# Turning attention weights and rows with VectorE and transfers in place of TensorE transposes

## The chip, the cores and the metric

The kernel runs on one core of a Trainium2 chip. A core has a matrix engine (TensorE, PE in the profile), a vector engine (VectorE, DVE), a scalar engine (ScalarE, ACT), a general engine (GpSimd, POOL) and a synchronisation engine (SyncE, SP). Each works through its own list of instructions in order; semaphores make one wait for another. SP issues the transfers of the weights; POOL issues those of intermediate data. The metric is the device time of one execution in microseconds.

## The reference

One decoder layer on 256 tokens of 2048 channels, in float32: a half-step gated feed-forward network (FFN), a token mixer of two attention branches, a second FFN, each followed by a layer norm.

```python
h = _layer_norm(ALPHA * x + 0.5 * _swiglu(x, ...), ...)
# mixer, with c_q, c_kv, k_r, dq, dk, dv, gate_mla, gate_diff = columns of h @ w_in
q = _rms_norm(c_q) @ w_uq              # 8 heads of 128, and 64 more that are rotated
k_nope, v = _rms_norm(c_kv) @ w_uk, _rms_norm(c_kv) @ w_uv
o_mla = softmax(q k^T * scale, causal) @ v                                   # 8 heads
o_diff = (softmax(s1) - lam * softmax(s2)) @ dv                              # 4 heads, 256 wide
o_diff = _rms_norm(o_diff, subln_g) * (1 - lambda_init)
y = sigmoid(gate_mla) * (o_mla @ w_br_mla) + sigmoid(gate_diff) * (o_diff @ w_br_diff)
out = y @ w_out
```

(The FFN and norm lines are shortened; the second FFN has the form of the first.)

## The kernel before

**Products.** A float32 product is made of three products of a shorter type: each operand is split into a high part (a cast, ACT, line 154) and a low part (a subtraction, DVE, line 155), and `triple` (lines 207 to 210) adds high x high, high x low and low x high in PSUM. The left operands are activations kept as columns, that is with channels on the partitions, in quads of four blocks of 128 channels (`Acts`); the right operands are weights, which arrive in chunks of 128 x 1024 (one *unit*: load, prepare, 12 products in two halves, b = 0 and 1, for the two blocks of 128 tokens).

**What sets the order.** The program is written unit by unit. `later(n, fn)` puts a piece of other work n units further on, and a scheduler orders each engine's list from that. Split weights lie in a ring of six pairs of tiles ("wring"); a pair can be written again when the products that read it are done. PSUM has five banks for products (`mm`) and three for the rest (`tr`). Short-lived tiles come from six slots ("tmp"), each taken again when its last reader is done; longer-lived ones from 41 slots ("act"). POOL's transfers rotate over eight semaphores: a transfer is issued when the one eight places ahead of it has landed.

**Turning rows into columns.** There are two ways. One is four transposes of PE into a PSUM bank (`rows_to_quad`, line 671; `p_cols`, line 1103). The other is `turn`: DVE transposes blocks of 32 x 32 within a tile ("blocks", line 715), POOL writes them to DRAM in four transfers ("turn", line 717) and reads them back later in one ("turned", line 729); ACT then copies or casts them (for kT, qT and qrT the copy of line 737). The order of channels that results is met by turned rows or columns of the weights, which the host lays out.

**The mixer.** After the columns of `w_in`, the two halves of attention share PE with the last gate projection, the projections of q (qT, and qr, which is rotated), k (kT) and v, and then the branch products. A differential head is four functions: scores (two softmaxes combined into p), `p_cols`, values (the result is normalised into "orow"), and a turn of orow by PE into "od". An MLA head is three: scores, `p_cols`, values into "om". Their distances are `later(2 + 6 * h + 3 * i + i // 3, f)` and `later(8 + 2 * h + 2 * i, f)`. For kT and qT, ACT copies the finished bank into a tile ("kTr", "qTr", line 1160), and DVE turns that tile a unit later. y is made by quads f = 0 to 3: the first two turn with `turn`, the last two with PE.

**The FFN.** The hidden rows hb are turned into DRAM (hT), and h is read back from it ("hraw", line 893) for the down projection.

Of the kernel before, what the change touches and what calls it, by code (L numbers as in the profile page):

```python
# [18 lines left out]
P = 128  # L19
# [40 lines left out]
def layer_kernel(ctx: ExitStack, tc: tile.TileContext, a: dict, out: bass.AP):  # L60
# [90 lines left out]
    cast, lows, fetched = [None], [None], [None]  # L151
# [560 lines left out]
    def turn_out(row, to):  # L712

        t = tmp_tile([P, 512], "blocks")
        V.transpose(t, row)  # L715
        for i in range(4):
            nc.gpsimd.dma_start(to.rearrange("(g r) (i f) -> i r g f", g=4, i=4)[i],  # L717
                                t[32 * i:32 * (i + 1), :].rearrange("r (g f) -> r g f", g=4))
# [4 lines left out]
    def turn(row, use, wait, more):  # L723
        to = dram.tile([P, 512], F32, name=nm("turn"))
        turn_out(row, to)

        def back():
            t = tmp_tile([P, 512], "turned")
            nc.gpsimd.dma_start(t, to)
            later(more, lambda: use(turned(t)))  # L730
        later(wait, back)

    def turn_to_quad(row, b, x, q, wait, more):
        turn(row, lambda t: x.put(q, b, t), wait, more)
# [117 lines left out]
    def ffn(n, x, wgu, wdn, residual, g, bt, each, first=None, between=None, nxt=None, cols=None, norm=None, pending=None):  # L852
# [7 lines left out]
        def half(c, b, up, gate, wait=0):  # L860
            q = c // 2
            sg = tmp_tile([P, 256], "sg")
            S.activation(sg, gate, AF.Silu)
            if c % 2 == 0:
                hb[b, q] = tmp_tile([P, 512], "hb")
            o = (c % 2) * 256

            def product():
                V.tensor_tensor(out=hb[b, q][:, o:o + 256], in0=up, in1=sg, op=ALU.mult)
            if wait:  # L870
                later(wait, product)
            else:
                product()
            if c % 2 == 1:
                later(12, lambda: put_h(b, q))
# [224 lines left out]
    def p_cols(p):  # L1100
        t = tr_bank()
        for i in range(3):
            PE.transpose(t[:, i * P:(i + 1) * P], p[:, i * P:(i + 1) * P], ident)
        pt = small.tile([P, 384], F32, tag="p", name=nm("pt"), bufs=3)
        S.copy(pt, t[:, 0:384])
        return pt

    def mixer(x):
# [76 lines left out]
        def pair_cols(w, name):  # L1185
            dst = [act_tile([P, 4, T], F32, name) for _ in range(2)]

            def done(n, b, bank, snap, op):
                t = tmp_tile([P, 512], name + "r")
                whole(t, bank, snap, op)  # L1190
                later(1, lambda: turn_to_cols(t, dst[n], b, 4, 10))
            hy.group(w[0], w[1], done, False, True)
            return dst
# [11 lines left out]
        def c_back(j):  # L1205
            if j == 0:
                for key, src in turns.items():
                    back[key] = tmp_tile([P, 512], "turned")
                    nc.gpsimd.dma_start(back[key], src)
# [7 lines left out]
        od = Acts(MH, "od")  # L1217

        def diff_head(h):
# [21 lines left out]
            def turn():  # L1241
                st["pt"] = p_cols(st["p"])

            def values():
# [14 lines left out]
                orow = tmp_tile([P, 512], "orow")  # L1259
                for b in range(2):  # L1260
                    V.scalar_tensor_tensor(out=orow[:, b * DV:(b + 1) * DV], in0=o[:, b * DV:(b + 1) * DV],
                                           scalar=r[:, b:b + 1], in1=subg, op0=ALU.mult, op1=ALU.mult)
                st["o"] = orow

            def turn2():
                t = tr_bank()
                for i in range(4):
                    PE.transpose(t[:, i * P:(i + 1) * P], st["o"][:, i * P:(i + 1) * P], ident)
                tv = t.rearrange("p (b i t) -> p b i t", b=2, i=2)
                for b in range(2):  # L1270
                    od.put(h // 2, b, tv[:, b], (h % 2) * 2, 2)
            return scores, turn, values, turn2
# [8 lines left out]
        def qr_done(b, bank):  # L1281
# [3 lines left out]
            later(1, lambda: turn_to_cols(t, qrT, b, 4, 10))  # L1285
        project(a["wuq"][2], cn, 4, 512, qr_done)
        kT = [cols_proj(a["wuk"][c], cn, 4, "kT", 4, 8) for c in range(2)]
# [6 lines left out]
        def mla_head(h):  # L1294
# [16 lines left out]
            def turn():  # L1311
                st["pt"] = p_cols(st["p"])
# [20 lines left out]
        for f, at in enumerate((16, 20, 28, 32)):  # L1333
# [11 lines left out]
        def branch_mla(f):  # L1345
# [5 lines left out]
            def done(b, bank):  # L1351
# [81 lines left out]
def _layout(i):  # L1433
# [28 lines left out]
    r["wbd"] = _chunks(w["w_branch_diff"], 512)  # L1462
    r["w_out"] = _chunks(np.concatenate([_turned_rows(w["w_out"][:1024]), w["w_out"][1024:]]), 512)
# [33 lines left out]
```

## Time and profile before

| | us |
|---|---|
| median of 3 runs | 1973.18 |
| lowest and highest | 1972.44, 1976.2 |
| profiled execution | 1972.85 |
| its span | 1971.1 |
| granted clock of PE in it | 0.998 |

A row of a group names line, engine, operation and tiles, then busy time, the mean of one in ns, and the idle time of the engine just before such instructions with what ended it. A row of a timeline begins with the start and the listed length; on PE lengths overlap, so that what an instruction costs is the distance to the next start. In the windows, each engine's busy time in a stretch is given with its number of instructions. A row of waits gives the time in all, how often, and the longest.

### The profile page before, as it was taken

How to read it: one execution, taken by the hardware profiler on the slowest of the kernel's cores; microseconds unless marked ns; L12 is line 12 of the kernel's file. 1: busy time of each engine (PE TensorE's matmuls, PEld its weight loads, DVE VectorE, ACT ScalarE, POOL GpSimd, SP SyncE). 2: the span in 40 equal slices, each digit the busy share in tenths (PEclk: the TensorE clock that was granted, in tenths of full speed). 3: DMA queues.
4: the chain of work that ended last, by engine and by line, in shares of the span. 5: the costliest groups of instructions: out<-in, count | busy, mean ns of one | idle time of the engine just before them, and what ended most of it. 6: DMA issues, size and time to landing. Idle time of an engine off the chain costs nothing.

```text
span 1971.1 us, 25747 instructions
## 1 busy us (share of the span) xinstructions
PE 1955.1 (99%) x8784; PEld 1620.0 (82%) x8784; DVE 1773.5 (90%) x2175; ACT 1265.5 (64%) x1650; POOL 291.0 (15%) x503
## 2 busy tenths in 40 slices
PE   9999999999999999999999999999999999999997
PEld 7888888888888898888888888888888888888886
DVE  7999999999998879988976677789999999999986
ACT  6666767676655566666667765556676776665661
POOL 0112111122100010102223120001211112210000
PEclk9999999999999999999999999999999999999999
DMA  8978888777776666767667668578888878786763
GB/s 309 287 227 262 285 270 251 235 216 281 296 235 222 209 218 254 244 224 259 223 198 241 234 216 271 199 263 254 254 263 294 243 243 249 238 321 237 274 234 124
DMA packets 147478, 485.71 MB, mean 246 GB/s; under 512 B 20961, under 2 KB 21009, under 8 KB 147345
## 3 DMA queue, kind: packets, MB, share of 16 engines
q1 hardware_dynamic: 117360, 397.99, 58.2%
q0 software_dynamic: 29984, 86.07, 16.4%
q8 instruction: 69, 1.13, 0.2%
q14 instruction: 65, 0.52, 0.1%
HBM read 455.13 MB, written 28.84 MB: 246 GB/s over the span
## 4 chain that ended last, share of the span: by engine, by line
PE 95%; DVE 2%; DMA 1%; issue 1%; ACT 0%; SPq 0%; DVEq 0%; ACTq 0%
PE mm L209 30%; PE mm L210 30%; PE mm L208 30%; DVE wring L155 1%; PE tr L208 1%; PE tr L210 1%; PE tr L209 1%; DMA sraw<-in_gu_dram 1%; PE tr L671 0%; DVE sraw L428 0%; ACT wring L154 0%; DMA raw<-in_gu_dram 0%; PE tr L1228 0%; PE tr L1301 0%; PE tr L1303 0%
## 5 line engine op out<-in xcount | busy, mean ns | idle before, releaser
L154 ACT CAST wring<-raw 128x1024 fp32r<-128x1024 f32 (+2 forms) x467 | 482.2, 1038 | 296.5 <-PE mm L210 207.2
L155 DVE TENSOR_TENSOR wring<-raw,wring 128x1024 fp32r<-128x1024 f32 (+2 forms) x467 | 559.1, 1206 | 95.4 <-ACT wring L154 92.8
L154 ACT CAST wring<-sraw 128x1024 fp32r<-128x1024 f32 x436 | 454.8, 1054 | 230.2 <-DVE sraw L428 94.2
L155 DVE TENSOR_TENSOR wring<-sraw,wring 128x1024 fp32r<-128x1024 f32 x436 | 523.2, 1228 | 21.6 <-ACT wring L154 18.8
L210 PE MATMUL mm<-wring,h 128*128 128x512 f32 (+2 forms) x1248 | 480.2, 385 | 0.0
L208 PE MATMUL mm<-wring,h 128*128 128x512 f32 (+2 forms) x1248 | 480.2, 385 | 0.0
L209 PE MATMUL mm<-wring,h 128*128 128x512 f32 (+2 forms) x1248 | 479.8, 385 | 0.0
L209 PE MATMUL mm<-wring,xs 128*128 128x512 f32 x776 | 302.2, 389 | 1.3 <-DVE wring L155 1.3
L208 PE MATMUL mm<-wring,xs 128*128 128x512 f32 x776 | 302.2, 389 | 0.0
L210 PE MATMUL mm<-wring,xs 128*128 128x512 f32 x776 | 302.0, 389 | 0.0
L209 PEld LDWEIGHTS mm<-wring,h 128*128 128x128 f32 x1248 | 234.5, 188 | 46.8 <-DVE wring L155 0.7
L210 PEld LDWEIGHTS mm<-wring,h 128*128 128x128 f32 x1248 | 234.5, 188 | 46.5 <-DVE h L155 0.7
L208 PEld LDWEIGHTS mm<-wring,h 128*128 128x128 f32 x1248 | 234.4, 188 | 46.4 <-ACT h L154 0.6
L428 DVE TENSOR_TENSOR sraw<-sraw,sraw 128x1024 f32<-128x1024 f32 x168 | 200.2, 1229 | 3.5 <-DMA sraw<-in_wdv_dram 1.6
L209 PEld LDWEIGHTS mm<-wring,xs 128*128 128x128 f32 x776 | 145.7, 188 | 32.5 <-DVE wring L155 2.3
L208 PEld LDWEIGHTS mm<-wring,xs 128*128 128x128 f32 x776 | 145.7, 188 | 30.1
L210 PEld LDWEIGHTS mm<-wring,xs 128*128 128x128 f32 x776 | 145.7, 188 | 30.0
L717 POOL DMA_DIRECT2D hT<-blocks x176 | 97.1, 562 | 370.0 <-DVE blocks L715 368.2
L208 PE MATMUL mm<-wring,x 128*128 128x512 f32 x336 | 130.8, 390 | 0.8 <-ACT wring L154 0.8
L209 PE MATMUL mm<-wring,x 128*128 128x512 f32 x336 | 131.0, 390 | 0.5 <-DVE wring L155 0.5
L210 PE MATMUL mm<-wring,x 128*128 128x512 f32 x336 | 130.6, 389 | 0.0
L430 POOL DMA_DIRECT2D sraw<-in_gu_dram x40 | 35.6, 900 | 359.4 <-DVE sraw L428 309.0
(307 smaller groups left out, 2289.6 us busy)
## 6 DMA issues: line engine op xcount, KB each, us to landing
sraw<-in_gu_dram SPq DMA_DIRECT2D x160, 512.0 KB, 5.4
raw<-in_gu_dram SPq DMA_DIRECT2D x159, 512.0 KB, 4.7
raw<-in_dn_dram SPq DMA_DIRECT2D x140, 512.0 KB, 4.7
sraw<-in_gu_dram POOLq DMA_DIRECT2D x40, 512.0 KB, 6.9
sraw<-in_dn_dram SPq DMA_DIRECT2D x36, 512.0 KB, 5.6
hraw<-hT POOLq DMA_DIRECT2D x68, 256.0 KB, 6.2
eraw<-in_gu_dram SPq DMA_DIRECT2D x64, 256.0 KB, 6.0
raw<-in_w_out_dram SPq DMA_DIRECT2D x32, 512.0 KB, 4.3
```

The costliest lines, as they stand in the source:

```text
L154: cast[0] = S.copy(hi, src)
L155: lows[0] = V.tensor_tensor(out=lo, in0=src, in1=hi.bitcast(F32), op=ALU.subtract)
L208: PE.matmul(o, xh, wh, start=first, stop=False, skip_group_check=again)
L209: PE.matmul(o, xh, wl, start=False, stop=False, skip_group_check=again)
L210: PE.matmul(o, xl, wh, start=False, stop=last, skip_group_check=again)
L428: last = V.tensor_tensor(out=R[src][i], in0=R[src][i], in1=R[add[1]][i], op=ALU.add)
L430: nc.gpsimd.dma_start(R["12"][s], source("22", s), accum_op=ALU.add)
L717: nc.gpsimd.dma_start(to.rearrange("(g r) (i f) -> i r g f", g=4, i=4)[i], t[32 * i:32 * (i + 1), :].rearrange("r (g f) -> r g f", g=4))
```

## The change

1. `p_cols` becomes `turn_p` for all 12 heads: DVE transposes p by blocks ("pblocks"), POOL writes it to DRAM ("pturn") and two units later reads it back in four transfers ("pt"), each for 32 partitions and made of 384 pieces of 32 numbers. The 36 transposes of PE and the 12 copies of ACT go.
2. A differential head has three functions. The normalised rows of two heads are kept in one pair of tiles, and after the second head `turn_to_quad` turns them: four turns of 128 x 512, and their casts and splits are four of 512 in place of eight of 256. The rows of `w_branch_diff` and all of `w_out` are laid out to match.
3. y's quads 2 and 3 use `turn_to_quad` too.
4. kT and qT are turned by DVE straight from their PSUM bank; the copies into kTr and qTr go, and with them the instruction that freed the bank.
5. The distances change: differential heads start 1 unit behind the call and 5 apart, MLA heads 3 units behind it (before: 8), turned tiles are used after 4 or 5 units in place of 8 or 10. Tiles read back for quads come from the act slots.
6. In the FFN, hb's product stands behind an earlier split, and h's reads stand behind the last turned-out transfer issued before them in the program.

```diff
     def turn_out(row, to):
         t = tmp_tile([P, 512], "blocks")
         V.transpose(t, row)
         for i in range(4):
-            nc.gpsimd.dma_start(to.rearrange("(g r) (i f) -> i r g f", g=4, i=4)[i],
+            turned_out[0] = nc.gpsimd.dma_start(to.rearrange("(g r) (i f) -> i r g f", g=4, i=4)[i],
                                 t[32 * i:32 * (i + 1), :].rearrange("r (g f) -> r g f", g=4))
...
-    def turn(row, use, wait, more):
+    def turn(row, use, wait, more, roomy=False):
...
-            t = tmp_tile([P, 512], "turned")
+            t = act_tile([P, 512], F32, "turned") if roomy else tmp_tile([P, 512], "turned")
...
             def product():
-                V.tensor_tensor(out=hb[b, q][:, o:o + 256], in0=up, in1=sg, op=ALU.mult)
+                with behind_split(3) if wait else nullcontext():
+                    V.tensor_tensor(out=hb[b, q][:, o:o + 256], in0=up, in1=sg, op=ALU.mult)
...
-            for b in range(2):
-                nc.gpsimd.dma_start(raw[:, b, :], hT[q, b])
+            with tc.issue_after(turned_out[0].ins):
+                for b in range(2):
+                    nc.gpsimd.dma_start(raw[:, b, :], hT[q, b])
...
-    def p_cols(p):
-        t = tr_bank()
-        for i in range(3):
-            PE.transpose(t[:, i * P:(i + 1) * P], p[:, i * P:(i + 1) * P], ident)
-        pt = small.tile([P, 384], F32, tag="p", name=nm("pt"), bufs=3)
-        S.copy(pt, t[:, 0:384])
-        return pt
+    def turn_p(p, keep, more, roomy=False):
+        t = tmp_tile([P, 384], "pblocks")
+        V.transpose(t, p)
+        to = dram.tile([P, 384], F32, name=nm("pturn"))
+        nc.gpsimd.dma_start(to, t)
+
+        def back():
+            pt = act_tile([P, 384], F32, "pt") if roomy else small.tile([P, 384], F32, tag="p", name=nm("pt"), bufs=3)
+            for k in range(4):
+                nc.gpsimd.dma_start(pt[32 * k:32 * (k + 1), :].rearrange("f (b i c) -> f b i c", b=3, i=4),
+                                    to.rearrange("(i f) (b k c) -> k f b i c", i=4, b=3, k=4)[k])
+            keep["pt"] = pt
+        later(more, back)
...
-        def cols_proj(w, xx, kt, name, k0=0, more=10):
+        def cols_proj(w, xx, kt, name, k0=0, more=5):
             dst = act_tile([P, 4, T], F32, name)
             def done(b, bank):
-                t = tmp_tile([P, 512], name + "r")
-                S.copy(t, bank)
-                later(1, lambda: turn_to_cols(t, dst, b, 4, more))
+                later(1, lambda: turn_to_cols(bank, dst, b, 3, more))
...
-                orow = tmp_tile([P, 512], "orow")
+                if h % 2 == 0:
+                    orows[h // 2] = act_tile([P, 2, 512], F32, "orow")
+                orow = orows[h // 2][:, :, (h % 2) * DV:(h % 2) * DV + DV]
...
-            def turn2():
-                t = tr_bank()
-                for i in range(4):
-                    PE.transpose(t[:, i * P:(i + 1) * P], st["o"][:, i * P:(i + 1) * P], ident)
...
+                if h % 2 == 1:
+                    rows = orows.pop(h // 2)
+                    for b in range(2):
+                        later(2 + b, lambda b=b: turn_to_quad(rows[:, b, :], b, od, h // 2, 2, 3))
...
-                later(2 + 6 * h + 3 * i + i // 3, f)
+                later(1 + 5 * h + (0, 3, 8)[i], f)
...
-        kT = [cols_proj(a["wuk"][c], cn, 4, "kT", 4, 8) for c in range(2)]
+        kT = [cols_proj(a["wuk"][c], cn, 4, "kT", 4, 4) for c in range(2)]
...
-                later(8 + 2 * h + 2 * i, f)
+                later(3 + 2 * h + (0, 2, 6)[i], f)
...
-                if f < 2:
-                    later(1, lambda: turn_to_quad(y[:, b, :], b, yq, f, 4, 6))
-                else:
-                    later(2, lambda: rows_to_quad(y[:, b, :], b, yq, f))
+                later(1, lambda: turn_to_quad(y[:, b, :], b, yq, f, *((4, 6) if f < 2 else (3, 3) if f == 2 else (1, 2))))
```

**Where instructions stand.** The first place is VectorE around the softmax of the last differential head, before (st is the scaled score, kTr the copied bank, raw a loaded weight):

```order
L715 STREAM_TRANSPOSE blocks_1048_8284<-kTr_1042_8272 128x512
L155 TENSOR_TENSOR wring_5_105<-raw_1159_8570,wring_4_104 128x1024
L715 STREAM_TRANSPOSE blocks_1060_8319<-kTr_1053_8308 128x512
L715 STREAM_TRANSPOSE blocks_1070_8356<-kTr_1063_8335 128x512
L155 TENSOR_TENSOR wring_3_103<-raw_1160_8587,wring_2_102 128x1024
L155 TENSOR_TENSOR wring_547_5086<-raw_1173_8631,wring_546_5085 128x1024
L155 TENSOR_TENSOR wring_19_119<-raw_1174_8648,wring_18_118 128x1024
L715 STREAM_TRANSPOSE blocks_1081_8386<-kTr_1076_8381 128x512
L155 TENSOR_TENSOR wring_17_117<-raw_1175_8666,wring_16_116 128x1024
L1257 TENSOR_SCALAR oms_1088_8418<-oss_1086_8414 128x2
```

and now, from head 1's normalised rows (orow) to the second half of kT (mm_1026_8221 and mm_1038_8260 are PSUM banks with k's first half for b = 0 and 1):

```order
L1272 SCALAR_TENSOR_TENSOR orow_949_8003<-tr_1003_8177,f_1013_8199,subg_97 128x256 x2
L1086 SCALAR_TENSOR_TENSOR st_1040_8270<-tr_1039_8267,bias3_94 128x384
L1086 SCALAR_TENSOR_TENSOR st_1047_8286<-tr_1046_8283,bias3_94 128x384
L1088 TENSOR_REDUCE mx_1041_8272<-st_1040_8270 128x1
L1089 TENSOR_REDUCE mx_1041_8272<-st_1040_8270 128x1
L155 TENSOR_TENSOR wring_17_117<-raw_1157_8526,wring_16_116 128x1024
L1091 TENSOR_SCALAR nmx_1042_8275<-mx_1041_8272 128x2
L715 STREAM_TRANSPOSE blocks_1057_8308<-orow_949_8003 128x512
L155 TENSOR_TENSOR wring_15_115<-raw_1159_8546,wring_14_114 128x1024
L715 STREAM_TRANSPOSE blocks_1061_8320<-mm_1026_8221 128x512
L1097 RECIPROCAL rs_1045_8281<-sums_1044_8278 128x2
L1088 TENSOR_REDUCE mx_1048_8288<-st_1047_8286 128x1
```

and directly on from there on the same engine:

```order
L1089 TENSOR_REDUCE mx_1048_8288<-st_1047_8286 128x1
L715 STREAM_TRANSPOSE blocks_1068_8345<-orow_949_8003 128x512
L1091 TENSOR_SCALAR nmx_1049_8291<-mx_1048_8288 128x2
L1097 RECIPROCAL rs_1052_8297<-sums_1051_8294 128x2
L715 STREAM_TRANSPOSE blocks_1071_8352<-mm_1038_8260 128x512
```

Before, DVE's turns of k read tiles that ACT had filled; now they read the banks, and stand between the turns of head 0 and 1's rows and the softmax of head 3.

The second place is POOL where differential head 2 (pturn_1017_8205, pt_1059_8314) is turned. Before, with no such transfers:

```order
L717 DMA turn_1038_8255<-blocks_1039_8256 32x4x128 x4
L729 DMA turned_1045_8281<-turn_980_8096 128x512
L717 DMA turn_1047_8283<-blocks_1048_8284 32x4x128 x4
L729 DMA turned_1057_8316<-turn_988_8123 128x512
L729 DMA turned_1067_8353<-turn_1026_8221 128x512
L717 DMA turn_1059_8318<-blocks_1060_8319 32x4x128 x4
L717 DMA turn_1069_8355<-blocks_1070_8356 32x4x128 x4
L729 DMA turned_1078_8383<-turn_1038_8255 128x512
```

Now:

```order
L1107 DMA pturn_1017_8205<-pblocks_1016_8203 128x384
L717 DMA turn_1021_8209<-blocks_1022_8210 32x4x128 x4
L729 DMA turned_1031_8241<-turn_985_8119 128x512
L717 DMA turn_1033_8243<-blocks_1034_8244 32x4x128 x4
L729 DMA turned_1054_8305<-turn_994_8146 128x512
L717 DMA turn_1056_8307<-blocks_1057_8308 32x4x128 x4
L1112 DMA pt_1059_8314<-pturn_1017_8205 32x12x32 x4
L717 DMA turn_1060_8319<-blocks_1061_8320 32x4x128 x4
L717 DMA turn_1067_8344<-blocks_1068_8345 32x4x128 x4
L717 DMA turn_1070_8351<-blocks_1071_8352 32x4x128 x4
```

The four reads of head 2's p stand behind the four writes of turn_1056_8307, which DVE's blocks_1057_8308 feeds, and ahead of the writes of turn_1067_8344.

The third place is ACT where v is copied from its banks (mm_1075_8368 before, mm_1086_8393 now, v's first half for b = 0). Before, ahead of head 2's values:

```order
L1160 COPY kTr_1042_8272<-mm_1031_8233 128x512
L1105 COPY pt_1056_8314<-tr_1055_8310 128x384
L154 CAST od_976_8088<-tr_1066_8344 128x256
L1290 COPY v_1072_8362<-mm_1075_8368 128x512
L154 CAST od_978_8092<-tr_1066_8344 128x256
L154 CAST wring_4_104<-raw_1159_8570 128x1024
L1160 COPY kTr_1053_8308<-mm_1044_8274 128x512
```

Now, behind the squares (junk) of head 2's values:

```order
L154 CAST wring_4_104<-raw_1174_8591 128x1024
L154 CAST wring_2_102<-raw_1182_8628 128x1024
L1263 ACTIVATE junk_1090_8411,oss_1089_8410<-tr_1088_8406 128x256 x2
L692 ACT_TABLE_LOAD
L692 ACTIVATE sd_1093_8418<-ve_1092_8416 128x2
L154 CAST wring_546_5085<-raw_1186_8652 128x1024
L154 CAST wring_18_118<-raw_1200_8699 128x1024
L1296 COPY v_1083_8387<-mm_1086_8393 128x512
```

The first copy of v stood between the turned p of a head and the casts of its rows; it now stands behind the squares, a table load, the root and two casts.

More of the change, by code (lines that the diff above doesn't have):

```diff
@@ L149, in at @@
             return self.tiles[k // 8, b][which][:, k % 8, :]
-    cast, lows, fetched = [None], [None], [None]
+    cast, lows, fetched, turned_out = [None], [None], [None], [None]
     def split(hi, lo, src):
@@ L733, in turn_to_quad @@
     def turn_to_quad(row, b, x, q, wait, more):
-        turn(row, lambda t: x.put(q, b, t), wait, more)
+        turn(row, lambda t: x.put(q, b, t), wait, more, True)
     def turn_to_cols(row, dst, b, wait, more):
@@ L1190, in done @@
                 whole(t, bank, snap, op)
-                later(1, lambda: turn_to_cols(t, dst[n], b, 4, 10))
+                later(1, lambda: turn_to_cols(t, dst[n], b, 4, 5))
             hy.group(w[0], w[1], done, False, True)
@@ L1206, in c_back @@
             if j == 0:
-                for key, src in turns.items():
-                    back[key] = tmp_tile([P, 512], "turned")
-                    nc.gpsimd.dma_start(back[key], src)
+                pairs = [act_tile([P, 2, 512], F32, "turned") for _ in range(2)]
+                for (i, b), src in turns.items():
+                    back[i, b] = pairs[i][:, b, :]
+                    nc.gpsimd.dma_start(back[i, b], src)
             if j >= 4:
@@ L1332, in get_gates @@
                     nc.gpsimd.dma_start(t[:, b, :], gate_rows[f, i, b])
-        for f, at in enumerate((16, 20, 28, 32)):
+        for f, at in enumerate((18, 20, 28, 32)):
             later(at, lambda f=f: get_gates(f))
```

19 lines of the change are left out of this document (8 added, 11 removed).

## The prediction

> **What bounds the kernel.** I read the page first, then the waits of TensorE (PE), then busy time by stage, then groups of instructions and landing times of transfers, and last the timelines of VectorE (DVE) and ScalarE (ACT) around the differential heads. The page:
>
> ```profile
> span 1971.1 us, 25747 instructions
> PE 1955.1 (99%) x8784; PEld 1620.0 (82%) x8784; DVE 1773.5 (90%) x2175; ACT 1265.5 (64%) x1650; POOL 291.0 (15%) x503
> PE 95%; DVE 2%; DMA 1%; issue 1%; ACT 0%; SPq 0%; DVEq 0%; ACTq 0%
> ```
>
> PE is the bound: busy 99% of the span, and 95% of the chain that ended last. A change can win only PE instructions that disappear and the little time that PE waits; it can lose whatever new time PE is made to wait. By stage, and the waits of PE:
>
> ```profile
> 100.00:685.00 585.00, 584.27 (x2577) 483.16 (x2575) 556.33 (x653) 383.67 (x474) 87.95 (x147) 1.00 0.77 249
> 1000.00:1050.00 50.00, 50.00 (x235) 41.71 (x234) 38.64 (x83) 33.20 (x61) 18.22 (x34) 1.00 0.68 217
> 1050.00:1085.00 35.00, 33.66 (x153) 27.17 (x152) 22.59 (x49) 27.96 (x51) 10.34 (x20) 1.00 0.72 243
> 1085.00:1150.00 65.00, 65.00 (x324) 54.73 (x323) 42.41 (x95) 54.47 (x99) 9.50 (x18) 1.00 0.59 206
> PE tr L1248 <- ACT pt L1105: 1.1, 1, 1.1
> PE tr L1103 <- DVE p L1237: 0.2, 1, 0.2
> ```
>
> Each stretch shows its length, then PE, weight loads, DVE, ACT, POOL (GpSimd). All that the heads cost PE in waiting is 35.00 - 33.66 = 1.34 us, 1.1 of it for a copied p (line 1105) and 0.2 for a p not yet scaled. DVE has slack in the mixer (22.59 of 35 us), none to speak of in the FFN (556 of 585).
>
> **What the change takes away.** 68 transposes of PE: 3 for each of 12 heads, 16 of the diff rows, 16 of y's last quads.
>
> ```profile
> L1103 PE MATMUL tr<-ident,p x36: 270/273/329, 999.0 to 1142.6; 128*128 128x128 f32 x36
> L1268 PE MATMUL tr<-ident,orow x16: 271/273/301, 1022.7 to 1085.2; 128*128 128x128 f32 x16
> L671 PE MATMUL tr<-ident,diff x16: 272/272/273, 1178.9 to 1194.2; 128*128 128x128 f32 x16
> 1042.61 0.27 PE L1103 MATMUL tr<-ident,p 128*128 128x128 f32 x1
> 1043.29 0.47 PE L208 MATMUL mm<-wring,cn 128*128 128x512 f32 x1
> 1043.61 0.39 PE L209 MATMUL mm<-wring,cn 128*128 128x512 f32 x1
> ```
>
> The listed 272 ns overlap in the pipeline, so the price is the distance: from 1042.61 seven transposes fill 0.68 us to the next product, which then starts its follower 0.32 after it. Seven cost between 0.68 and 0.78, some 0.10 to 0.11 each; 68 x 0.109 = 7.4 us. PE's 1.34 us of waiting goes too, since what it waited for is gone: together -8.7 us. The 12 copies of p and the 8 of kTr and qTr are worth nothing by themselves: ACT is busy 54 of 65 us there, and it is 0% of the chain.
>
> ```profile
> 392.83 4.41 POOL L717 DMA_DIRECT2D hT<-blocks  x8 [14.49 <-DVE blocks L715]
> hraw<-hT POOLq DMA_DIRECT2D x68, 256.0 KB, 6.2
> L208 PE MATMUL mm<-wring,h x1248: 277/389/580, 455.3 to 1959.6; 128*128 128x512 f32 x169, 128*128 128x256 f32 x5, 128*128 128x320 f32 x5
> ```
>
> POOL's part in the FFN is priced at nothing: h's first reads move behind the hT writes that end at 397 us, take 6.2 us to land, and PE first reads h at 455. An hb product that stands three splits later has that same cover (PE waits 0.73 us in that whole stretch); if the cover fails, it costs at worst one split of 1.13 us (priced below) in each of ten groups of an FFN, some 20 us in both, which I leave outside the range.
>
> **What it adds on POOL.** Each head writes p's blocks once to DRAM and reads them back in four transfers of 32 x 12 x 32. That is 60 issues, besides 40 for the diff rows and y. DVE gains 12 turns of p and 8 of rows at 0.64 or less (priced below), 13 us at most in 150 of which it is idle 46; what of them stands in PE's way is counted further down. For the issues, the nearest rows:
>
> ```profile
> L717 POOL DMA_DIRECT2D turn<-blocks x104 | 56.8, 554 | 168.3 <-DVE blocks L715 139.8 <-DVE ms L1126 18.4 <-DVE nmx L1089 6.7
> L729 POOL DMA_DIRECT2D turned<-turn x22 | 12.3, 558 | 35.5 <-DMA turn<-blocks 16.2 <-DVE rs L1095 4.1 <-ACT qT L737 3.2
> L430 POOL DMA_DIRECT2D sraw<-in_gu_dram x40 | 35.6, 900 | 359.4 <-DVE sraw L428 309.0 <-PE mm L210 47.1 <-issue 2.8
> turned<-turn POOLq DMA_DIRECT2D x26, 256.0 KB, 4.3
> gate<-gates POOLq DMA_DIRECT2D x16, 256.0 KB, 7.4
> DMA to landing us min/median/max: 1.9/3.4/5.2
> ```
>
> The last row is of the blocks that are turned in the mixer. An issue takes 0.55 us with 128 pieces, 0.90 at the dearest. The new reads have 384 pieces of 128 bytes, which no row shows: from 0.55 (pieces free) to 3 x 0.55 = 1.65 (all of it pieces). I take 0.8, between the two rows shown, and 4.3 us to land, from the reads that come back as these do.
>
> [...]
>
> **What it moves onto the path.** kT and qT are now turned by DVE straight from their PSUM bank. Before, an ACT copy freed the bank; now DVE's turn frees it, in DVE's order. There are five banks, so the bank of k's first half (mm_8221 for b = 0, mm_8260 for b = 1; a tile is named by its last number) is wanted again by v: mm_8462 (first half, b = 1), mm_8476 and mm_8513 (second half), and then by the gate projection, mm_8530. DVE's and ACT's rows that price the queue:
>
> ```profile
> 1041.13 0.42 DVE L1074 TENSOR_TENSOR qr<-ropes,ropec 128x256 f32<-128x256 f32 x1
> 1042.58 0.71 DVE L715 STREAM_TRANSPOSE blocks<-qr 128x512 f32<-128x512 f32 x1
> 1043.21 2.32 DVE L155 TENSOR_TENSOR wring<-raw,wring 128x1024 fp32r<-128x1024 f32 x2
> 1053.78 1.53 DVE L715 STREAM_TRANSPOSE blocks<-kTr 128x512 f32<-128x512 f32 x2 [5.12 <-DMA turn<-blocks]
> 1063.96 0.88 DVE L1261 SCALAR_TENSOR_TENSOR orow<-tr,f,subg 128x256 f32<-128x256 f32 x2
> 1064.76 1.01 DVE L1084 SCALAR_TENSOR_TENSOR st<-tr,bias 128x384 f32<-128x384 f32 x2
> 1065.69 0.28 DVE L1086 TENSOR_REDUCE mx<-st 128x1 f32<-128x128 f32 x1
> 1065.88 0.41 DVE L1087 TENSOR_REDUCE mx<-st 128x1 f32<-128x256 f32 x1
> 1066.20 1.22 DVE L155 TENSOR_TENSOR wring<-raw,wring 128x1024 fp32r<-128x1024 f32 x1
> 1071.43 0.17 DVE L1095 RECIPROCAL rs<-sums 128x2 f32<-128x2 f32 x1 [1.08 <-ACT p L1093]
> 1076.75 1.04 ACT L154 CAST wring<-raw 128x1024 fp32r<-128x1024 f32 x1
> 1079.87 0.39 ACT L1254 ACTIVATE junk<-tr 128x256 f32<-128x256 f32 x1
> 1081.66 1.28 ACT L692 ACT_TABLE_LOAD   x1
> L1290 ACT COPY v<-mm 128x512 f32<-128x512 f32 x4 | 2.4, 591 | 3.7 <-PE mm L210 3.7
> 1059.80 0.23 PE mm L208
> ...
> 1066.60 0.23 PE mm L208
> ```
>
> The row at 1053.78 shows the danger already: a turn of kT waited 5.12 us for a block tile that POOL's transfers still held. Then ACT's copy had freed the bank and PE did not notice. I price by distances of starts, as the rows follow each other: a turn 0.64, a split 1.13 to 1.16, the pair of orow 0.80, of st 0.93, the two mx 0.51, a qr 0.37, a row of 128x2 elements 0.1 (0.2 where one waits for the other).
>
> *First bank.* I start both sides at the product that frees the weight buffer of raw_8502. PE has 31 more products to the first one of mm_8462, at 0.227 us each (30 between the last two rows, in 6.80 us): 7.0 us. On the other side: cast 1.05, split 1.13, then in DVE's order the rest of the rope (two qr, 0.74), three dependent rows of head 1's root (0.6), blocks_8244 (0.64), orow (0.80), two st (0.93), mx (0.51), split (1.13), nmx (0.1), blocks_8308 (0.64), split (1.13), and blocks_8320, which frees the bank (0.64): 10.0, with some 0.1 for each of four changes of engine 10.4. PE waits 3.4 us. blocks_8320 also needs blocks_8244's tile back; its fourth write starts some 1.7 us after blocks_8244 and lands 3.4 later, which is just hidden; at 5.2 it adds 1.7, and with all of DVE's handovers free the wait is 3.0.
>
> *Second bank.* mm_8476 comes 7 products (1.6 us) later and wants blocks_8352. After blocks_8320 DVE does mx (0.51), blocks_8345 (0.64), nmx and rs (0.2), waits 1.08 for ACT's exponentials, turns (0.7): 3.2. PE waits 1.6. A third bank (mm_8513, behind two more splits) costs 0.4.
>
> *v's copy.* mm_8530 wants a bank that ACT frees by copying v. ACT stands before that at the squares of head 2's values, whose scratch tile is held by blocks_8345 until POOL's four writes land. Counted from blocks_8320's end (blocks_8308 ended 1.8 before): four writes 2.2, four pt reads 3.2, four writes 2.2; the last write of blocks_8345 waits for its semaphore, which is free when the transfer eight places ahead, the last pt read, has landed (at 2.8 + 4.3 = 7.1), and lands at 10.5. Then squares 0.75, root's input and pblocks 0.8 beside a table load (1.28), root 0.2, two casts 2.0, the copy 0.6: 15.3. PE gets there at 1.6 + 1.6 + 17 x 0.227 + 1.3 (head 2's values) + 0.4 + 12 x 0.227 = 11.5. It waits 3.8; with the writes at 1.9 us to land 2.3, at 5.2 us 5.6.
>
> *The pieces of p themselves.* Counted along the queues in the same way, at 0.55 us per issue, the differential heads 0 to 3 have them 6, 1, 0.5 and 1.5 us before PE wants them, MLA's heads 0 to 6. At 0.8 the MLA heads 3 to 5, whose reads alternate with the next head's write, come 0.7 late in all; at 1.65 all of them together 6 or more. y's quads 2 and 3 land 2 to 3 us before w_out wants them, and od's halves 1 us: nothing.
>
> **The sum**, against the profiled execution of 1972.85 (span 1971.1 and 1.75 around it; the median of the runs is 1973.18): -7.4 - 1.3 + 3.4 + 1.6 + 0.4 + 3.8 + 0.7 = +1.2, that is 1974.1 us. Measurements of this kernel tell 0.2% (4 us) from no change, so I forecast no measurable change: the transposes are saved, and given back at PSUM banks.
>
> **Rivals.** *The banks are free in time* (faster). If DVE and ACT run ahead of what I counted by the 3 to 4 us of slack that 22.59 of 35 busy leaves, the first and the v wait vanish and 1.6 + 0.4 stay at most: 1972.85 - 8.7 + 0 to 2 = 1964 to 1966. For it: DVE's idle time. Against it: the queue is in order and its start hangs on a cast that PE itself releases.
>
> *Pieces are dear* (slower). At 1.65 us per read, four reads take 6.6: diff head 1 is 0.5 late, head 2 2.3, the v wait grows by 3, MLA heads 3 to 5 wait about 2 each: 1974.1 + 9 = 1983. It decides from about 1.2 us on (1977). For it: three times the pieces. Against it: the 0.90 row, twice the bytes for less than twice the time.
>
> *Small pieces land late* (slower). At 7 us instead of 4.3 each pt read is 2.7 later: head 2 by 2.2, the v wait by 2.7, the MLA heads about 2: 1981. For it: reads of gates take 7.4 in this stage. Against it: reads of turned blocks, which the new ones resemble, take 4.3.
>
> **How the numbers follow.** Forecast case 0.42 (1970 to 1978), banks free 0.25, dear pieces 0.23, late landing 0.10. Faster by over 0.2% is below 1969.2: the second case and a little of the first, 0.28. Slower is above 1977.1: the last two and a little of the first, 0.35. Between: 0.37. The range goes from 1965, most of the faster case, to 1986, dear pieces with writes at 5.2 us; the likeliest case alone has 1970 to 1978.
>
> **What would show it.** Right: PE's waits name DVE blocks (the turns) and ACT v, some 5 and 4 us, between 1065 and 1090; 68 transposes fewer; pt reads at 0.6 to 1.0 us on POOL; no wait of PE in the FFN or at w_out. Wrong: those two waits under 1 us each (then the first rival), values of the heads waiting for pt by more than 3 us in all (one of the others, told apart by issue and landing), or any new PE wait before 1000 us, which I have priced at nothing.

## The result, and the profile after

The changed kernel takes 1989.9 us (median of four runs, 1987.1 to 1990.8) against 1973.0 before: ratio 1.008, 95% interval 1.0062 to 1.0097. The forecast was 1974.1, no measurable change, in a range from 1965 to 1986. The change is 17 us slower, outside the range.

The page of the changed kernel, first lines and the chain that ended last; behind it its list of what PE waited for (total, times, longest):

```profile
span 1987.7 us, 25775 instructions
PE 1956.0 (98%) x8716; PEld 1615.6 (81%) x8716; DVE 1782.5 (90%) x2191; ACT 1239.5 (62%) x1616; POOL 350.7 (18%) x603
...
PE 86%; DMA 5%; DVE 4%; issue 2%; POOL 1%; ACT 1%; SPq 0%; DVEq 0%; POOLq 0%; ACTq 0%
```

```profile
PE mm L208 <- DVE blocks L715: 5.1, 2, 3.3
PE mm L208 <- ACT y L154: 4.9, 3, 4.3
PE mm L209 <- DVE wring L155: 3.8, 6, 1.7
PE mm L208 <- ACT v L1296: 2.3, 1, 2.3
PE mm L210 <- DVE y L155: 1.8, 1, 1.8
...
PE tr L1323 <- DMA pt<-pturn: 0.5, 2, 0.3
```

All 68 transposes are gone (8784 matmuls to 8716), yet PE is busy as long as before: 1956.0 us against 1955.1. Its idle time grew from 16.0 to 31.7 us. The first and fourth wait are the ones forecast. The y waits and the wring wait are not. Why busy time did not fall by the 7.4 us that the transposes were priced at is seen, in the main, in the windows of 2 us around the wait that ended at 1048.5 (length, then the busy time of PE, weight loads, DVE, ACT and POOL, then PE's granted clock, the transfer engines' share and GB/s):

```profile
1046.00:1048.00 2.00, 0.00 (x0) 0.00 (x0) 2.00 (x4) 1.25 (x5) 1.03 (x2) 1.00 0.63 229
1048.00:1050.00 2.00, 1.53 (x4) 1.26 (x5) 1.64 (x6) 0.33 (x2) 1.08 (x3) 0.71 1.03 361
1050.00:1052.00 2.00, 1.92 (x5) 1.07 (x4) 1.27 (x5) 1.47 (x5) 2.00 (x5) 0.50 0.67 228
1052.00:1054.00 2.00, 2.00 (x9) 1.60 (x9) 2.00 (x5) 0.24 (x1) 2.00 (x5) 0.94 0.49 104
```

After PE has stood still here, its products follow each other every 0.43 us instead of 0.227, for some 3.4 us, at a granted clock of 0.50. Behind the copy of v the half clock begins 1.5 us after the wait has ended, and behind y's it lasts over 5 us. Summed over the products that are 0.40 to 0.43 us apart, this costs 1.0 us behind the wait at 1048, 1.6 behind the copy of v and 2.4 behind y's. With the slow products beside them (the first ones behind a wait, and two that are 0.71 and 0.56 us apart behind the first) it is 1.9, 1.8 and 3.3, which is 7 of the 8.3 us that PE is busy longer than with 7.4 us of transposes gone.

Where the time went is read best from the shift of the same product between two kernels. This table is worked out from the starts of PE's products; its columns are times of the kernel before:

| shift against before, us, at | 400 | 470 | 990 | 1160 | 1240 | end |
|---|---|---|---|---|---|---|
| forecast | 0 | 0 | 0 | +2.9 | +1.2 | +1.2 |
| after | -1.8 | +0.8 | +1.1 | +6.7 | +15.6 | +16.6 |
| y and FFN undone (below) | -0.6 | -0.6 | -0.5 | +8.8 | +9.6 | +9.7 |
| MLA part alone (below) | -0.2 | -0.2 | -0.5 | -2.2 | -1.7 | -1.7 |

The shift at 400 differs between -2.1 and +0.9 over all kernels run, changed there or not, and says nothing. From there the changed kernel loses 2.6 us by 470, about where the first FFN's down projection begins, 5.6 in the heads, 8.9 at y, about 1 in the second FFN. Of the heads' 5.6 some 2.6 is half clock by the first sums (1.0 + 1.6) and 3.6 by the second. These are readings of one execution: in those of four other kernels with the same heads (runs below) the heads lose 5.1 to 9.3 us, and y 6.8 to 10.9 in three with the same y.

What happens at y, in POOL's timeline of the changed kernel and in the chain:

```profile
1204.86 1.63 POOL L717 DMA_DIRECT2D turn<-blocks  x3 [0.98 <-DVE blocks L715]
1209.90 0.56 POOL L729 DMA_DIRECT2D turned<-turn  x1 [3.41 <-issue]
1210.44 0.55 POOL L717 DMA_DIRECT2D turn<-blocks  x1
1217.72 0.56 POOL L729 DMA_DIRECT2D turned<-turn  x1 [6.72 <-DMA turn<-blocks]
```

```profile
1210.44 6.70 DMA turn<-blocks
...
1217.72 6.14 DMA turned<-turn
```

The fourth write of the last row stands behind a read that waits 3.41 us for an earlier row. That row's own writes took up to 6.0 us to land, and its read 6.4: w_out's first half on quad 3 starts at 1217.0, after a wait of 4.25 us. The fourth write takes 6.70 us to land, and the read behind it 6.14: the second half starts at 1224.6.

### The profile page after: what moved, and what is told of

It is laid out like the page before. It is cut to its first block, busy times and chain, and to the rows that moved or that the text cites. A ratio compares the mean times of both kernels' runs of the same rounds, so it can differ in the third digit from the quotient of the medians.

```text
span 1987.7 us, 25775 instructions
## 1 busy us (share of the span) xinstructions
PE 1956.0 (98%) x8716; PEld 1615.6 (81%) x8716; DVE 1782.5 (90%) x2191; ACT 1239.5 (62%) x1616; POOL 350.7 (18%) x603
## 4 chain that ended last, share of the span: by engine, by line
PE 86%; DMA 5%; DVE 4%; issue 2%; POOL 1%; ACT 1%; SPq 0%; DVEq 0%; POOLq 0%; ACTq 0%
PE mm L209 27%; PE mm L210 27%; PE mm L208 27%; DVE wring L155 2%; DMA turn<-blocks 1%; DMA turned<-turn 1%; DMA sraw<-in_gu_dram 1%; PE tr L209 1%; PE tr L210 1%; PE tr L208 1%; DVE sraw L428 1%; DMA pt<-pturn 1%; POOL turn L717 1%; ACT wring L154 1%; DMA gate<-gates 0%
```

## The experiments

All ratios are to the kernel before, with 95% intervals; single parts are judged by medians (about +-2 us).

**1. y by PE again, and the FFN edits away.** Apart, then together:

```diff
-later(1, lambda: turn_to_quad(y[:, b, :], b, yq, f, *((4, 6) if f < 2 else (3, 3) if f == 2 else (1, 2))))
+if f < 2:
+    later(1, lambda: turn_to_quad(y[:, b, :], b, yq, f, 4, 6))
+else:
+    later(2, lambda: rows_to_quad(y[:, b, :], b, yq, f))
...
-r["w_out"] = _chunks(_turned_rows(w["w_out"]), 512)
+r["w_out"] = _chunks(np.concatenate([_turned_rows(w["w_out"][:1024]), w["w_out"][1024:]]), 512)
```

> The changed kernel, but y's quads 2 and 3 are transposed by PE again (16 transposes, 1.7 us) and w_out's rows stand for that. Theory (the two reads of y that come back late cost 7 us of waiting at w_out, and the half clock behind the longer wait 2 to 3 us more): the nth product's lag of 15.6 us behind y falls to 6 or 7, PE waits name no y, and the time is about 1981 (1979 to 1983). Rival (the reads are not the bound there: w_out's first loads or the norm behind them would keep PE waiting instead): 1987 or more.

```diff
-with behind_split(3) if wait else nullcontext():
+with nullcontext():
...
-with tc.issue_after(turned_out[0].ins):
+with nullcontext():
```

> The changed kernel without its two edits in the FFN (h's first quads asked for late, h's products behind three splits). Theory (the FFN edits cost what the shift of the products shows there, some 0.7 in the first FFN and 1.0 in the second, beside 1.8 won before): about 1988, between 1986 and 1990, and the shift from 462 us on gone. Rival (these edits cost nothing, as the prediction priced them; the 1.7 comes from w_in's order and from differences of execution): 1989.5 and the same shift.

> The changed kernel with y's quads by PE and without the FFN edits, both at once: what is left is the heads. Theory (the two parts add up, 6.7 and 2.1 measured apart): 1981 (1979 to 1983), so that the heads alone make the kernel some 8 us slower than before. Rival (one of them had hidden the other): 1985 or more.

Measured: 1983.2 (1.0053, 1.0040 to 1.0065), 1987.8 (1.0070, 1.0056 to 1.0084) and, with both, 1981.3 (1.0039, 1.0027 to 1.0052). The parts add up: 6.7 and 2.1 make 8.8, and both together give 8.6. So the heads alone cost some 8 us. Without the FFN edits the shift at 470 is that at 400. Which of the two FFN edits costs the 2 us was not separated.

**2. y alone, on the kernel before.**

> The kernel before, with only y's quads 2 and 3 turned by DVE and transfers (16 transposes of PE less, 1.7 us). Theory (the fourth write of the last turn stands on POOL behind a read that waits for the turn before it, and then lands 6 to 7 us later, whatever the heads did): 1972.9 - 1.7 + 7 of waiting + 2 to 3 of half clock = about 1981 (1978 to 1983). Rival (they came late only since the mixer's POOL work was late by then): 1971 to 1973, and no wait of PE for y.

Measured 1986.4 (1.0064, 1.0052 to 1.0077). The rival falls: with the mixer's POOL work as before, y's turned quads cost 13 us by themselves, more than they cost inside the change. It is also 3 us more than the theory's range. The waits of PE and the chain, from the slowest of its five executions (1989.8):

```profile
PE mm L208 <- ACT y L154: 11.2, 3, 5.4
```

```profile
1208.37 6.95 DMA turn<-blocks
...
1215.89 7.08 DMA turned<-turn
```

Both halves of quad 3 wait over 5 us here. The four writes of the last row follow each other without a read between them this time, so the theory's detail is not the cause either. Write and read each take 7 us while w_out's weights arrive, where the prediction counted 3.4 and 4.3.

**3. Keeping PE busy through the wait at y.**

```diff
+if (b, j) in fill:
+    tf = tr_bank()
+    for i in range(34):
+        PE.matmul(tf[:, 0:P], zero, zero, start=True, stop=True)
```

(`fill` is set for the first half of w_out's first unit on quad 3.)

> The changed kernel with 34 products of zeros more (128x128, some 3.7 us, results used nowhere) ahead of w_out's first product on y's quad 3, where PE waited 4.6 us and then ran 12 products at half clock. Theory (it is PE's idleness that halves the clock): the products after the wait follow each other every 0.23 us again instead of 0.43, no granted clock of 0.50 behind 1217 us, and 2.4 us are won: about 1987.5. Rival (the clock falls with the burst of transfers or by a period of its own): the half clock stays, 1990.

PE's timeline of that run (x68: each product counts twice):

```profile
1213.83 7.75 PE L224 MATMUL tr<-zero 128*128 128x128 f32 x68
1221.34 0.48 PE L208 MATMUL mm<-wring,y 128*128 128x512 f32 x1
1221.65 0.40 PE L209 MATMUL mm<-wring,y 128*128 128x512 f32 x1
...
1227.28 0.50 PE L208 MATMUL mm<-wring,y 128*128 128x512 f32 x1 [1.61 <-ACT y L154]
```

Measured 1991.3 (1.0093, 1.0079 to 1.0108): no gain, though the granted clock is 1.00 in every window of 2 us from 1210 to 1226 us and over the whole of 1200 to 1235, with the transfer engines as busy as in the changed kernel (1.02 to 1.04 from 1216 to 1226). So in this run, at this place, it is PE's idleness that halves it (0.50 there in the changed kernel), not the burst of transfers. But the fill took 7.75 us, twice what I had expected, and PE then waited again for the second half of quad 3. The stage from 1160 to 1240 us ends with that last read: it lost 8.9 us in the changed kernel and 8.7 here. Behind y the half clock cost nothing that could be won here, because a later arrival covered it.

**4. The banks copied out by ACT again.**

```diff
-later(1, lambda: turn_to_cols(bank, dst, b, 3, more))
+t = act_tile([P, 512], F32, name + "r")
+S.copy(t, bank)
+later(1, lambda: turn_to_cols(t, dst, b, 3, more))
```

> The changed kernel, but ACT copies q and k out of their PSUM banks as before, and DVE turns the copy (8 copies more on ACT, none on PE). Theory (the banks held by DVE's turns cost 5.1 us of waiting, and the first of these waits, 3.3 us, also halves the clock for some 3.4 us, which is 1.5 us): the waits named DVE blocks vanish, the time is about 1983 (1981 to 1985). Rival (the copies come as late on ACT, or ACT's later copy of v grows by as much): 1988 to 1990, with the waits now named ACT.

The waits of PE in that run:

```profile
PE tr L1259 <- DMA pt<-pturn: 6.9, 1, 6.9
PE mm L208 <- ACT y L154: 5.1, 2, 4.5
PE tr L1325 <- DMA pt<-pturn: 3.8, 2, 2.3
PE mm L208 <- ACT kTr L1169: 2.3, 1, 2.3
```

Measured 1991.7 (1.0093, 1.0080 to 1.0106). The theory falls: the waits named DVE blocks are gone, and others as long or longer stand in their place. So the bank is not the only thing that PE would have to wait for in this stage.

**5. One part of the heads at a time, on the kernel before.** The MLA part (24 transposes of p, banks turned directly, early distances); the differential part (12 transposes of p, 16 of rows, banks copied); the rows alone:

> The kernel before with only the MLA heads' part: p of 8 MLA heads by DVE and transfers (24 transposes less, 2.6 us), heads 3 units behind v, k and q turned straight from their banks, qT and kT back earlier. Diff heads, y and FFN as before. Theory (DVE's turns hold the banks whatever the diff heads do): two waits named DVE blocks of 5 us together, 1.5 of half clock, the copy of v and pieces 1 or 2: 1973 - 2.6 - 0.2 + 7.5 = about 1977 (1975 to 1980). Rival (the bank waits come from the diff heads' new work on DVE and POOL): 1969 to 1971.

> The kernel before with only the diff heads' part: p of 4 diff heads by DVE and transfers, diff rows turned too (28 transposes less, 3.1 us), each head 5 units behind the one before, ACT copying q and k out of their banks. MLA heads, y and FFN as before. Theory (without the bank waits p's pieces come back in time but for one): 1973 - 3.1 - 1.3 + 0 to 3 = about 1970 (1968 to 1972). Rival (the heads' pieces are late by themselves, as with the banks copied: a wait for pt of 5 us and more, with half clock): 1975 to 1979.

> The kernel before with only the 8 rows of the diff heads turned by DVE and transfers (16 transposes of PE less, 1.7 us), heads 5 units apart; p stays with PE. Theory (the rows land in time, as the prediction priced them): 1971 (1970 to 1972), no wait for od. Rival (the block tiles and POOL's four writes per row push p and q behind, as the row of before with 5.12 us for a block tile suggests): 1974 to 1977.

Measured: 1972.7 (1.0000, 0.9990 to 1.0009), 1987.4 (1.0066, 1.0054 to 1.0078) and 1981.3 (1.0041, 1.0029 to 1.0053). All three theories fall. Turning q and k straight from their banks costs next to nothing by itself: PE waits for no bank in the MLA run, though of the 2.6 us that its 24 transposes are priced at the median shows only 0.3. (This part also reads the first gates back at unit 18 in place of 16, an edit of the change that is not in its list.) In the differential part PE waits 10.4 us for one head's pieces of p. The rows, which the prediction had priced at nothing beyond their turns in the queue of the banks, cost 8 us alone. (They are 4 rows, 16 writes and 4 reads; the expectations speak of 8 rows, 32 writes and 18 us of POOL, which is twice too many.) With the rows alone PE waits for these:

```profile
PE mm L208 <- ACT v L1288: 5.5, 1, 5.5
PE mm L208 <- ACT kTr L1160: 2.4, 1, 2.4
```

The second is a wait for a bank, though ACT copies the banks out there; it ends at 1050.3 us, and what made it is not shown. For the first, which ends at 1060.5, what holds ACT is seen in its timeline, at the squares of the head's result, in the run with the rows alone and in that of the whole differential part:

```profile
1057.11 0.38 ACT L1255 ACTIVATE junk<-tr 128x256 f32<-128x256 f32 x1 [3.84 <-DMA turn<-blocks]
```

```profile
1072.60 0.38 ACT L1273 ACTIVATE junk<-tr 128x256 f32<-128x256 f32 x1 [19.26 <-DMA turn<-blocks]
```

The squares want one of the six scratch tiles. It is held by blocks whose writes have not landed, and behind the squares ACT's copies of v, q and k wait. Not all of the idle time is the tile's: the head's values are there at about 1055.0 and 1064.0 us by PE's timeline, so that the tile costs some 2 and 8.5 us.

**6. What about the rows costs the 8 us: distances, POOL's time, or the tiles?** Only the distances; the distances and 16 spare writes at the same places of the program; the rows with blocks, read-back tile and squares outside the ring.

```diff
-later(2 + 6 * h + 3 * i + i // 3, f)
+later(1 + 5 * h + 3 * i, f)
```

> The kernel before with the diff heads begun one unit earlier and five units apart instead of six, nothing else (all transposes on PE). Theory (the rows and pieces cost, not where the heads stand): 1973, within 2. Rival (heads that stand closer run into ACT's and DVE's queue by themselves): 1978 and more, as far as the rows alone went (1981).

> As the run before, with 32 writes more on POOL at the places where the diff rows' blocks are written (128 pieces of 512 bytes as there, from v of the diff heads, to memory that nobody reads; no DVE turn, no scratch tile, no read back). Theory (what is held are scratch tiles and in-order queues behind them, not POOL's time): as without these writes, within 2. Rival (18 us of POOL's issue time and the transfers beside push k's and q's turns back): 1978 to 1982.

```diff
-t = tmp_tile([P, 512], "blocks")
+t = act_tile([P, 512], F32, "blocks") if roomy else tmp_tile([P, 512], "blocks")
...
-junk = tmp_tile([P, 512], "junk")
+junk = act_tile([P, 512], F32, "junk")
```

> The kernel before with the diff rows turned (as the run of the rows alone, 1981), but blocks, rows read back and the squares' scratch in tiles of their own, outside the ring of six. Theory (the ring): PE waits at v vanish, 1973 - 1.7 = about 1971.5 (1970 to 1974). Rival (POOL's queue order and the head distances are enough): 1978 to 1981.

Measured: 1971.2 (0.9992, 0.9983 to 1.0001), 1971.1 (0.9991, 0.9982 to 1.0000), 1974.4 (1.0012, 1.0003 to 1.0021). The closer distances cost nothing, and own tiles take 6.9 of the rows' 8.3 us away. The run with spare writes does not test what it was meant to: they wait for nothing that the heads make, and POOL issued them long before the heads' full stage (lengths in ns, then the first and the last start in us):

```profile
L1276 POOL DMA_DIRECT2D spare<-dv x16: 551/551/567, 973.9 to 984.5; - x16
```

In the run with the rows alone, DVE turns the rows at 1031, 1039 and 1083 us. It is the run with own tiles that decides: it keeps all 16 writes and 4 reads of POOL and changes only where tiles lie. The ring of scratch tiles is what the rows ran into, and not POOL's time. The ring is still short in that run: PE waits 3.3 us for a bank while DVE's turn of k waits 3.5 us for a block tile.

**7. p of all heads, rows by PE; then with own tiles.**

> As the run before, but the diff rows go back to PE (16 transposes); p of all 12 heads stays with DVE and transfers (36 transposes less than before, 3.9 us), MLA heads early, k and q turned from their banks. Theory (the diff rows' 32 writes on POOL, and the scratch tiles that they hold, are what makes PE wait): 1973 - 3.9 + 1 to 2 = about 1970.5 (1968 to 1972.5), no wait of 2 us at v. Rival (p's pieces of the diff heads share POOL's queue with k's turns and are enough): 1977 and more.

> p of all heads by DVE and transfers, diff rows, y and FFN as before, and the squares' scratch outside the ring. Theory: 1970 (1968 to 1972), as without own scratch, since with no row writes the ring isn't held long. Rival (the ring is short even so): 1 to 2 us less than without.

> p of all 12 heads by DVE and transfers as in the run that measured 1980 (diff rows, y and FFN as before), but p's blocks, p read back and the squares' scratch in tiles of their own. Theory (the ring of six scratch tiles and that of three tiles for p hold the heads up): 1970 to 1973. Rival (for p it is the time of the trip: DVE's turn, a write, POOL's four reads and 5 to 6 us to land, against two units of distance): 1977 to 1981.

Measured: 1980.4 (1.0030, 1.0020 to 1.0040); with the squares alone outside the ring 1982.0 (1.0044, 1.0031 to 1.0058); with p's blocks, p read back and the squares outside 1974.3 (1.0008, 0.9999 to 1.0017). The rows are not the only ones to run out of tiles: own tiles for p and the squares together are worth 6.1 us, those of the squares by themselves none. Whether p's blocks or the three tiles that p is read back into are the short ones was not separated.

**8. Parts put together.** All the heads with own tiles for rows and squares; the MLA part and the rows; the MLA part and the closer distances, with no differential transfer at all:

> The heads as changed, y and FFN as before, but the blocks of rows that are turned and the scratch of the squares have tiles outside the ring of six scratch tiles. Theory (PE waits since the ring's tiles are held until POOL's writes land: squares, k's turns and the copy of v stand behind that): the second bank wait and the copy of v, 2 to 3 us each, and the half clock behind go; the first bank wait of 3.3 us, where DVE turns rows ahead of k, stays: 5 us less than without own tiles, about 1976 (1974 to 1978). Rival (POOL's order of issues alone holds them up): 1980 to 1983.

> p of the MLA heads and the diff rows turned, own tiles as in the run before, p of the diff heads, y and FFN as before (40 transposes less, 4.4 us). Theory: if own tiles free the rows, 1969 to 1971, faster than both kernels. Rival (k's turns from the banks stand behind the rows' turns on DVE, 3.3 us and half clock): 1975 to 1978.

> Two parts that cost nothing each, put together: p of the MLA heads by DVE and transfers (24 transposes less, 2.6 us; measured 0 apart) and the diff heads five units apart with all their transposes on PE (measured 2 us faster apart). Theory (they add up): 1970.5 (1968 to 1972.5), a little faster than both kernels. Rival (either uses up the same slack of ACT and DVE between 1030 and 1065 us): 1974 to 1980, with waits for v or a bank.

Measured: 1979.0 (1.0033, 1.0020 to 1.0045), 1977.0 (1.0023, 1.0014 to 1.0032) and 1978.7 (1.0032, 1.0020 to 1.0044). The first is between theory and rival, 2.2 us below the same heads without own tiles (1981.3), out of the 8 that they cost: p's blocks are still in the ring. The heads with own tiles for rows, squares and p at once were not run. In the second, PE waits for DVE at 1048 and 1060 us again (3.5 and 2.3 us), with half clock behind both (1000 to 1100 us: granted clock 0.97, against 1.00 before): own tiles do not free the banks where DVE turns rows as well. The third was meant to be the best version and is 6 us slower than before, though each half alone costs nothing. Its waits, in the fastest of its six executions (1976.1):

```profile
PE tr L1333 <- DMA pt<-pturn: 4.1, 3, 2.8
...
PE mm L208 <- ACT v L1306: 0.7, 1, 0.7
PE tr L671 <- DVE diff L1370: 0.7, 1, 0.7
```

So the two parts seem to use the same slack. Through which queue is open: the run shows pieces of p that are late in the MLA heads, not what made them late. None of these versions beats the kernel before by more than can be measured; the closer distances alone, with the spare writes or without, come lowest, at 0.9991 and 0.9992.

## Why the prediction was wrong, point by point

- **y's quads 2 and 3 "land 2 to 3 us before w_out wants them ... nothing".** This step failed most. For that stage -1.7 us was forecast and +8.9 measured, which is 10.6 of the 15.4 us missed in this execution; undoing y gave 6.7 us back, which with the 1.7 makes 8.4 of the 15.8 missed in the medians. The landings were taken from the mixer's rows (3.4 and 4.3 us); in w_out's stage they are 6 to 7, with the transfer engines busy to 0.94 from 1210 to 1224 us, where the mixer has 0.77 from 1050 to 1085. y alone confirms the place (+13). That the busy engines make the landings slow is argued: no run changed their load by itself. The trace of the changed kernel fits it, since its 64 KB writes of turned blocks land in 2.1 us (median of 26) where the engines were busy under 0.6 of that time, and in 4.4 (of 75) where it was over 0.8; but 6 to 7 is long even among those.
- **The FFN edits priced at nothing.** Undoing them gives 2.1 us back. The prediction had named the place (a wait for a split) and left it outside the range.
- **First, second and third bank, 3.4, 1.6 and 0.4 us; v's copy, 3.8; pieces of p, 0.7.** Measured 3.3, 0.1, 1.8; 2.3; 1.1. The first bank came as counted. The second is ready late too, but PE, at half clock, comes later. The third is late for a reason that the prediction had for v alone, a scratch tile that is not free; DVE's turn of the bank and ACT's squares both wait for the landing of blocks:

  ```profile
  1058.35 0.72 DVE L715 STREAM_TRANSPOSE blocks<-mm 128x512 f32<-128x512 f32 x1 [1.27 <-DMA turn<-blocks]
  ```

  ```profile
  1059.65 0.39 ACT L1263 ACTIVATE junk<-tr 128x256 f32<-128x256 f32 x1 [3.83 <-DMA turn<-blocks]
  ```

  That the total is so near the forecast is partly luck, then. And the heading under which the prediction put the bank waits, "what it moves onto the path" by the turn from the bank, tells half of the cause. Undoing that turn won nothing, and the MLA part, which has it, cost nothing; the rows alone brought a wait for a bank with ACT as its copier. The shortage is of the whole stage: the "13 us at most in 150" of DVE and the POOL issues were counted, the time for which tiles are held was not.
- **No term for the clock.** A wait was priced at its length. The waits in the heads came to 8.8 us, 1.1 less than the 9.9 forecast; the half clock behind two of them adds 2.6 to 3.6 us. Together that is 1.5 to 2.5 of the 2.7 us between +2.9 forecast and +5.6 measured. The granted clock of the changed kernel is 0.50 from 1048.82 to 1052.23 us, behind the wait of 3.28 us, and from 1065.89 to 1069.30, behind that of 2.31 us; that of the kernel before is 1.00 in every stretch listed from 1000 to 1150 us.
- **-7.4 us for 68 transposes.** They went, as counted; the MLA run, with 24 of them, comes out 1.7 us shorter in its profile (0.3 in the median).
- **The rivals.** Banks free in time: refuted, 5.1 us of waits. Pieces dear: refuted; four pieces of p per head take this, against the 0.8 us assumed and 1.65 feared (the group of the issues in the changed kernel, mean in ns, then its list of transfers, median to landing):

```profile
L1112 POOL DMA_DIRECT2D pt<-pturn x48 | 32.0, 716 | 13.8 <-PE mm L210 5.4 <-DMA pturn<-pblocks 4.0 <-DMA turned<-turn 1.8
```

```profile
pt<-pturn POOLq DMA_DIRECT2D x48, 48.0 KB, 4.8
```

  Small pieces late at 7 us: not for p (4.8), but the figure fits y's large ones. (The sum of the dear pieces was added low: the delays that it lists make 11 us, not 9, if none lies within another.)
- **"Any new PE wait before 1000 us" and waits at w_out** were named as what would show it wrong. Both came.

## What to carry to other kernels

Price a transfer's landing by landings of the stage where it will run, and look at what else the transfer engines move there; its kind is not enough (here 3.4 and 4.3 us in the mixer, 6 to 7 for the last rows of y). When transposes of PE give way to turns and transfers, count for how long each scratch tile is then held, and who takes the next one: parts that fit one by one can fail together (here two parts that cost nothing apart came out 6 us slower together). In the changed kernel waits of PE of 3.28 and 2.31 us cost 1.0 to 1.9 us more in clock; at y, where a later arrival came behind the half clock, keeping PE busy won nothing. And look in the trace whether the work that an experiment adds ran where it was meant to run.

## What the runs showed of the hardware that was not expected

- In the changed kernel an issue of 384 pieces of 128 bytes takes POOL 0.72 us, one of 128 pieces of 512 bytes 0.55 to 0.58: three times the pieces, 0.15 us more.
- 16 spare writes of POOL, of 64 KB each, issued between 974 and 985 us, ahead of the heads' full stage, cost nothing (1971.1 against 1971.2 us).
- In these runs the length of a wait does not tell whether half clock follows. In the changed kernel it followed one of 2.31 us; with the rows in own tiles PE's wait of 3.28 us, which ended at 1056.4, left the clock at 1.00 (windows of 2 us of that run):

```profile
1054.00:1056.00 2.00, 0.00 (x0) 0.00 (x0) 0.99 (x4) 0.26 (x1) 0.05 (x1) 1.00 0.77 301
1056.00:1058.00 2.00, 1.62 (x7) 1.36 (x8) 1.73 (x5) 1.82 (x4) 2.00 (x4) 1.00 0.32 88
```
